# Seven block products for eight in the feed-forward input layers of a two-block model

## The chip, the cores and the metric

One core of a Trainium2 chip runs the whole program. The metric is the device time of one execution in microseconds (us); lower is better. PE is the matmul engine (TensorE), PEld its weight loads, DVE the vector engine (VectorE), ACT the scalar engine, POOL GpSimd, SP the queue that issues the weight transfers.

## The reference

Two model blocks on 512 tokens of width 1024, all in fp32. Each block has mixers (state space, attention, gating; then dilated attention and mLSTM) and feed-forward layers; there are three of these, called f1, f2 and f3 below. All three compute

```python
FF_HIDDEN = 2816
a, b = jnp.split(h @ w_in, 2, axis=-1)      # w_in: 1024 x 5632
f = (jax.nn.silu(a) * b) @ w_out            # w_out: 2816 x 1024
```

## The kernel before

Every fp32 operand of a large product is kept as two fp32r pages, a high half (`hi`, a rounded copy that ACT makes, L300) and a low half (`lo`, what is left, that DVE makes, L306), and each product is three matmuls: high by high (L315), high by low (L316), low by high (L317). That is `mm3`.

`swiglu` runs a feed-forward layer in two parts of 11 groups. A group is one pair of outer tiles: 128 columns of `a` and the 128 columns of `b` that belong to them. `linear_fm` computes a group: the weights come in two slabs (`raw`, 4 tiles of 128 rows by 256 columns, one transfer for each pair member), are split into `whi` and `wlo`, and stand as stationary operand; the 512 tokens of `xT` stream past. A group has 2 outer tiles x 8 row tiles x 3 = 48 matmuls of 512 columns into two PSUM banks. At the start of a layer the first two groups are computed in two passes of 256 tokens each (`half` 0 and 1), since the second half of the tokens is normalized late. At a group's end ACT applies Silu (L901), DVE multiplies (L902), and the result `hid` is split at once (L300, L306). After 11 groups the down-projection (`resid`, by `linear_tm` or, at f1's end, `linear_pairs`) uses `hid` as stationary and streams `w_out`.

Each engine runs its instructions in the order in which the program writes them. `tick` writes one piece of PE work, and after it the evacuations that the piece before left behind; `slab` fetches weights: transfers up to six slabs ahead, splits up to three. SBUF work pages come from a pool of 36, PSUM has 8 banks.

Of the kernel before, what the change touches and what calls it, by code (L numbers as in the profile page):

```python
# [9 lines left out]
F32 = mybir.dt.float32  # L10
F32R = mybir.dt.float32r
# [5 lines left out]
P = 128  # L17
# [64 lines left out]
class Lin:  # L82


    keep = 0

    def __init__(self, w, K, groups, kind, kt, k0=0, rot=0):
        self.w = w.rearrange("(k p) n -> p k n", p=P)
# [7 lines left out]
    def chunks(self):  # L96
        return [(k, min(self.kt, self.KT - k)) for k in range(0, self.KT, self.kt)]

    def specs(self):
        for gi, ents in enumerate(self.groups):  # L100
            n = sum(e[1] for e in ents)
            ch = self.chunks()
            for k, kk in ch[: len(ch) - self.keep] if gi else ch:
# [10 lines left out]
                yield srcs, kk, n, self.rot  # L114


class XT:
# [13 lines left out]

    def __getitem__(self, k):
        return self.tiles[k // 4][:, k % 4]


class LateXT(XT):
# [109 lines left out]
class Core:  # L246
# [5 lines left out]
    def __init__(self, tc, ins, out, dbg=None):  # L252
        self.tc = tc
        self.nc = tc.nc
        self.ins = ins
        self.out = out
        self.dbg = dbg
        self.n = 0
        self.pend = []
        self.bgs = []  # L260
        self.now = 0.0
        self.left = None
        self.specs = []
        self.i_raw = self.i_split = self.i_use = 0
        self.raws, self.splits = {}, {}
        self.los = []

    def nm(self, s):
        self.n += 1
# [55 lines left out]
    def prefetch(self, n_raw, n_split):  # L325
        nc = self.nc
        n_raw, n_split = min(n_raw, len(self.specs)), min(n_split, len(self.specs))
        while self.i_split < n_split or self.i_raw < n_raw:
            if self.i_raw < n_raw and self.i_raw - self.i_split < self.RAW:
                srcs, kt, n, _ = self.specs[self.i_raw]  # L330
                raw = self.page(name="raw")
                rv = raw[:, : kt * n].rearrange("p (k n) -> p k n", k=kt)
                for off, w, ap in srcs:
                    nc.sync.dma_start(rv[:, :, off : off + w], ap)
                self.raws[self.i_raw] = raw
                self.i_raw += 1
            elif self.i_split < n_split:
                i = self.i_split
                srcs, kt, n, rot = self.specs[i]
# [12 lines left out]
                self.i_split += 1  # L352
            else:
                break

    def slab(self, lin, idx, ahead=2):
# [5 lines left out]
        self.i_use += 1  # L362
        return self.splits.pop(i)

    def run_los(self):
        los, self.los = self.los, []
        for f in los:
            f()


    def tick(self, emit, evacs=(), cost=1.0, soon=()):
# [8 lines left out]
        for f in list(soon) + self.pend:  # L380
            f()
        self.pend = list(evacs)
        for b, n in ns:
# [9 lines left out]
            f()  # L393
        self.pend = []

    def linear_fm(self, lin, xT, evac, groups=2):


        idx = 0
# [20 lines left out]
        if self.left:  # L420
# [16 lines left out]
                    )  # L437
            post.finish(range(NT))
            self.left = None
            for gi, ents, ps, ci, k0, kk, hl in work:  # L440
# [5 lines left out]
        for gi in range(first, len(lin.groups)):  # L446
            ents = lin.groups[gi]
            ps = [self.ps("fm") for _ in ents]
            for ci, (k0, kk) in enumerate(ch):
# [4 lines left out]
                for mi, a, n in steps:  # L454
# [3 lines left out]
                        [lambda gi=gi, ps=ps: evac(gi, ps)] if last else (),  # L458
                        cost=n / 4,
                    )  # L460

    def linear_tm(self, lin, xT, evac, tail=2, post=None):

# [3 lines left out]
        for gi, ents in enumerate(lin.groups):  # L467
# [20 lines left out]

            while len(ch) - done > tail:
                k0, kk = ch[done]  # L490
                if isinstance(xT, LateXT):
                    xT.need(k0)
# [4 lines left out]
                done += 1  # L497
            sl = []
            for k0, kk in ch[done:]:
                if isinstance(xT, LateXT):  # L500
                    xT.need(k0)
                sl.append((k0, kk, self.slab(lin, idx)))
                idx += 1
            for t in range(NT):
# [16 lines left out]
    def linear_pairs(self, lin, xT, evac, post):  # L521
# [14 lines left out]
        for p in range(2):  # L536
# [3 lines left out]
            tail = lin.keep if p == 0 else self.TAIL_PAIR  # L540
            sl = []
            for k in ks:
                if p and k >= lin.KT - lin.keep:
                    s = kept[k - lin.KT + lin.keep][1]
                else:
# [253 lines left out]
    def plan_all(self):  # L799
# [3 lines left out]
        def pair(c0, n):  # L803
            return [[(c0 + 256 * g, P), (c0 + 256 * g + P, P)] for g in range(n)]

        def fm(name, w, K, groups, kt=4, k0=0, rot=0):
            L[name] = self.plan(Lin(w, K, groups, "fm", kt, k0, rot))

        def tm(name, w, K, groups, kt=2, k0=0, keep=0):
            L[name] = Lin(w, K, groups, "tm", kt, k0)  # L810
# [6 lines left out]
        def ffn(name, w_in, w_out):  # L817
            for part in range(2):
                j0 = part * nh
                fm(f"{name}i{part}", w_in, D, [[((j0 + j) * P, P), (FFH + (j0 + j) * P, P)] for j in range(nh)])  # L820
# [72 lines left out]

    def swiglu(self, name, xT, h, gain, first, post=None, stats=None):
        nc = self.nc
        for part in range(2):
            hid = []
# [9 lines left out]
            self.linear_fm(self.L[f"{name}i{part}"], xT, ev, self.HALF_F1 if name == "f1" else 2)  # L907
# [5 lines left out]
            self.flush()  # L913

    def rms_post(self, h, gain_row, name, order="same", fp32_out=None):

# [1397 lines left out]
class Block2(Block1):  # L2314
# [14 lines left out]
    FIN1 = 23  # L2329
    MLSTM_RATE = 2.5  # L2330
    HALF_F1 = 2
    PAIRS = ("f1",)
    KEEP = 3
    TAIL_PAIR = 4
# [869 lines left out]
```

## Time and profile before

| | us |
|---|---|
| time, median of 3 runs (lowest, highest) | 2498.6 (2497.31, 2502.82) |
| the profiled execution's own time | 2498.47 |
| its span, first to last instruction | 2496.8 |
| PE busy | 2414.6, 97% |
| DVE busy | 1292.4, 52% |

The time is the span and some 1.7 us around it. PE busy is the time in which a matmul was in the array, and says nothing of how fast matmuls follow each other; that is read from the starts of consecutive rows.

### The profile page before, as it was taken

What the parts mean: (1) busy time and instruction counts of PE and PEld (TensorE: products, weight loads), DVE (VectorE), ACT (ScalarE), POOL (GpSimd) and SP (SyncE); (2) the same over time, 40 slices, a digit from 0 to 9 for tenths busy, and PEclk for the clock granted to TensorE, in tenths of its full rate; (3) what the DMA queues carried; (4) which work ended last, traced back from release to release, by engine and by line L of the source; (5) the groups of instructions that cost most, each with busy time, mean ns of one, the idle gap of its engine ahead of it and who ended that gap; (6) DMA issues with size and microseconds to landing.
All of it is one profiled execution on the core that took longest, in us unless ns stands there. A gap on an engine that the chain in (4) does not pass through costs nothing.

```text
span 2496.8 us, 30987 instructions
## 1 busy us (share of the span) xinstructions
PE 2414.6 (97%) x11960; PEld 1991.2 (80%) x11960; DVE 1292.4 (52%) x2161; ACT 964.4 (39%) x1666; POOL 307.9 (12%) x345
## 2 busy tenths in 40 slices
PE   6989999997999999999999999999999999999998
PEld 5877776677878888888888888888888777888887
DVE  6768736686444367455545563323355566433233
ACT  4345446632221234555445543312233454322231
POOL 2025412104000001121011200000001231000000
PEclk8989999998999999999999999999999999999999
DMA  8255651353333243332333242232241214324321
GB/s 298 83 173 169 212 181 58 119 183 105 110 110 94 80 137 105 93 85 76 110 85 91 88 128 85 89 114 85 85 135 36 58 60 136 100 80 119 88 80 48
DMA packets 330916, 272.79 MB, mean 109 GB/s; under 512 B 28178, under 2 KB 286630, under 8 KB 330768
## 3 DMA queue, kind: packets, MB, share of 16 engines
q1 hardware_dynamic: 323764, 252.36, 33.1%
q0 software_dynamic: 3344, 9.78, 1.1%
q10 hardware_dynamic: 3660, 8.66, 0.9%
q8 instruction: 94, 1.54, 0.3%
q14 instruction: 54, 0.44, 0.1%
HBM read 253.45 MB, written 13.09 MB: 107 GB/s over the span
## 4 chain that ended last, share of the span: by engine, by line
PE 82%; DVE 7%; ACT 2%; issue 1%; POOL 1%; DMA 0%; DVEq 0%; ACTq 0%; POOLq 0%
PE fm L315 17%; PE fm L316 16%; PE fm L317 16%; PE tm L315 8%; PE tm L317 8%; PE tm L316 8%; DVE wlo L306 1%; PE ao L2575 1%; PE as L2449 1%; PE tr L750 1%; PE apt L2551 0%; PE ms L1841 0%; PE mo L1903 0%; DVE rq_t L630 0%; ACT mT L296 0%
## 5 line engine op out<-in xcount | busy, mean ns | idle before, releaser
L315 PE MATMUL fm<-xT,whi 128*128 128x512 f32 (+1 forms) x1744 | 664.6, 381 | 0.3 <-ACT xT L300 0.2
L317 PE MATMUL fm<-xT,wlo 128*128 128x512 f32 (+1 forms) x1744 | 658.5, 378 | 4.4 <-DVE wlo L306 4.4
L316 PE MATMUL fm<-xT,whi 128*128 128x512 f32 (+1 forms) x1744 | 657.3, 377 | 0.8 <-DVE xT L306 0.7
L306 DVE TENSOR_TENSOR wlo<-raw,whi 128x1024 fp32r<-128x1024 f32 (+4 forms) x445 | 488.6, 1133 | 87.8 <-ACT whi L300 69.7
L300 ACT CAST whi<-raw 128x1024 fp32r<-128x1024 f32 (+3 forms) x447 | 393.4, 920 | 143.8 <-PE tm L316 51.1
L317 PEld LDWEIGHTS fm<-xT,wlo 128*128 128x128 f32 x1744 | 331.8, 190 | 66.9 <-DVE wlo L306 4.6
L315 PEld LDWEIGHTS fm<-xT,whi 128*128 128x128 f32 x1744 | 332.5, 191 | 61.5 <-issue 1.7
L316 PEld LDWEIGHTS fm<-xT,whi 128*128 128x128 f32 x1744 | 332.1, 190 | 60.5 <-DVE xT L306 1.4
L902 DVE TENSOR_TENSOR sl<-sl,fm 128x512 f32<-128x512 f32 x66 | 45.4, 688 | 425.5 <-PE fm L317 413.0
L315 PE MATMUL tm<-whi,hid 128*128 128x512 f32 x528 | 208.4, 395 | 0.0
L317 PE MATMUL tm<-whi,hid 128*128 128x512 f32 x528 | 207.7, 393 | 0.0
L316 PE MATMUL tm<-wlo,hid 128*128 128x512 f32 x528 | 207.5, 393 | 0.0
L901 ACT ACTIVATE sl<-fm 128x512 f32<-128x512 f32 x66 | 39.5, 599 | 382.2 <-PE fm L317 382.2
L317 PEld LDWEIGHTS tm<-whi,hid 128*128 128x128 f32 x528 | 99.1, 188 | 23.2
L316 PEld LDWEIGHTS tm<-wlo,hid 128*128 128x128 f32 x528 | 99.2, 188 | 22.8
L315 PEld LDWEIGHTS tm<-whi,hid 128*128 128x128 f32 x528 | 99.1, 188 | 22.8
L315 PE MATMUL tm<-whi,xT 128*128 128x384 f32 (+1 forms) x320 | 114.5, 358 | 0.0
L300 ACT CAST hid<-sl 128x512 fp32r<-128x512 f32 x66 | 41.0, 621 | 187.0 <-DVE sl L902 187.0
L317 PE MATMUL fm<-hT,wlo 128*128 128x512 f32 x256 | 103.9, 406 | 8.5 <-DVE wlo L306 8.5
L317 PE MATMUL tm<-whi,xT 128*128 128x384 f32 (+1 forms) x320 | 112.1, 350 | 0.0
L316 PE MATMUL tm<-wlo,xT 128*128 128x384 f32 (+1 forms) x320 | 111.7, 349 | 0.0
L315 PE MATMUL fm<-hT,whi 128*128 128x512 f32 x256 | 105.3, 411 | 0.3 <-ACT whi L300 0.3
(596 smaller groups left out, 3434.7 us busy)
## 6 DMA issues: line engine op xcount, KB each, us to landing
raw<-in_ffn_w_in_dram SPq DMA_DIRECT2D x264, 256.0 KB, 3.4
raw<-in_ffn_w_out_dram SPq DMA_DIRECT2D x69, 512.0 KB, 3.6
raw<-in_attn_w_in_dram SPq DMA_DIRECT2D x96, 256.0 KB, 3.3
adaw<-in_w_ada_dram SPq DMA_DIRECT2D x40, 512.0 KB, 6.8
raw<-in_w_in_dram SPq DMA_DIRECT2D x36, 512.0 KB, 7.8
raw<-in_attn_w_in_dram SPq DMA_DIRECT2D x96, 128.0 KB, 2.6
raw<-in_mlstm_w_in_dram SPq DMA_DIRECT2D x24, 512.0 KB, 3.7
gates<-gt ACTq DMA_DIRECT2D x12, 512.0 KB, 5.5
```

The lines of the kernel that those rows point to most:

```text
L300: nc.scalar.copy(hi, src)
L306: f = lambda: eng.tensor_tensor(lo, src, hi.bitcast(F32), op=ALU.subtract)
L315: nc.tensor.matmul(out, a[0], b[0], start=start, stop=False)
L316: nc.tensor.matmul(out, a[0], b[1], start=False, stop=False)
L317: nc.tensor.matmul(out, a[1], b[0], start=False, stop=stop)
L750: self.nc.tensor.transpose(ps[:, (k - k0) * P : (k - k0 + 1) * P], src[:, k * P : (k + 1) * P], self.ident)
L901: nc.scalar.activation(s, ps[0], AF.Silu)
L902: nc.vector.tensor_tensor(s, s, ps[1], op=ALU.mult)
L2449: nc.tensor.matmul(ss[:, rs], q[:, rs], k[:, rs], start=True, stop=True)
L2575: nc.tensor.matmul(ov[:, :, r, :], vs[1][:, r, g - 1, :], t3(pts[1 + g][:, rs]), start=g == 1 and r == 0, stop=False,)
```

## The change

36 of the 66 groups are computed in another way: in f1 the groups 4, 6, 8, 10 of the first part and 0, 2, 4, 6, 8, 10 of the second; in f2 and f3 the groups 4, 5, 7, 8, 10 of the first part and 0, 1, 3, 4, 6, 7, 9, 10 of the second. For such a group the weights are four blocks of 512 rows x 128 columns (row half by pair member), the tokens four blocks of 512 rows x 256 tokens. Instead of eight block products there are seven, of sums and differences of blocks (Strassen's scheme in the form with shared sums). Three parts are new:

- `win_prep`, per group: DVE forms the weight sums S1 to S4 in place; ACT and DVE split the seven blocks.
- `win_x`, once per layer: DVE adds the halves of `xT` back together, forms the token sums T1 to T4 and splits them; both parts use them.
- `win_pair`: seven products of 12 matmuls of 256 columns (84 for 48 of 512) in three PSUM banks `wa`, `wb`, `wc`, each bank two halves; DVE adds them up as they finish, ACT applies Silu, DVE multiplies.

The preparations are generators in a list `jobs`; `tick` takes one step of them for each 0.51 of cost, from 1.3 groups ahead. `hid` is kept unsplit (`Hidden`, two groups to a page) and is split in 1024-wide pieces when the down-projection is two pairs away, the first ones during the part's last group. The other 30 groups run as before (`std_group`).

```diff
+    def win_prep(self, i):
+        self.prefetch(i + 4, i + 2)
+        r1, r2 = self.raws.pop(i), self.raws.pop(i + 1)
+        s = self.page(name="ws")
+        q = self.t2(name="wq")
+        v = lambda pg: pg.rearrange("p (m k n) -> p m (k n)", m=2, k=4)
+        v1, v2, vs = v(r1), v(r2), v(s)
+        tt(vs, v2[:, 0].unsqueeze(1).to_broadcast([P, 2, 512]), v1, op=ALU.subtract)
...
+        high("1", r1)
+        yield
+        tt(v2[:, 0], v1[:, 0], vs[:, 1], op=ALU.subtract)
+        tt(q, v2[:, 1], v2[:, 0], op=ALU.subtract)
+        yield
+        low("1", r1)
+        high("2", r2)
+        yield
+        low("2", r2)
+        high("s", s)
+        yield
+        low("s", s)
+        qr = self.page([P, 2, 512], F32R, "wqs")
+        nc.scalar.copy(qr[:, 0], q)
+        yield
+        tt(qr[:, 1], q, qr[:, 0].bitcast(F32), op=ALU.subtract)
...
+    def win_pair(self, i, tx, store):
+        w = self.win.pop(i)
+        a, b, c = self.ps("wa"), self.ps("wb"), self.ps("wc")
...
+        def prod(out, wn, xn):
+            for k in range(4):
+                self.mm3(out, (wh[:, k], wl[:, k]), (xh[:, k], xl[:, k]), k == 0, k == 3)
...
+        def first():
+            nc.scalar.copy(x1, half(b, 0))
+        def sum_11():
+            v(y[:, 0:2], two(a), twice(x1), op=ALU.add)
+        def sum_w():
+            v(y[:, 2], y[:, 1], half(b, 1), op=ALU.add)
+        def sum_22():
+            v(y[:, 1::2], y[:, 1:3], twice(half(b, 0)), op=ALU.add)
+        def out():
+            v(y[:, 1:3], y[:, 1:3], two(c), op=ALU.add)
+            f = y.rearrange("p c n -> p (c n)")
+            nc.scalar.activation(f[:, :512], f[:, :512], AF.Silu)
+            v(store(), f[:, :512], f[:, 512:], op=ALU.mult)
+        seq = [
+            (half(b, 0), "A11", "B11", [first]),
+            (half(a, 1), "S2", "T2", []),
+            (half(a, 0), "A12", "B21", [sum_11]),
+            (half(b, 1), "S3", "T3", [sum_w]),
+            (half(b, 0), "S1", "T1", [sum_22]),
+            (half(c, 0), "S4", "B22", []),
+            (half(c, 1), "A22", "T4", [out]),
+        ]
+        for j, (o, wn, xn, ev) in enumerate(seq):
+            self.tick(lambda: prod(o, wn, xn), ev, cost=0.51)
...
             def ev(gi, ps):
                 s = self.t2(name="sl")
                 nc.scalar.activation(s, ps[0], AF.Silu)
-                nc.vector.tensor_tensor(s, s, ps[1], op=ALU.mult)
-                pg = self.split_page("hid")
-                self.split(pg[:, 0, :], pg[:, 1, :], s)
-                hid.append(pg)
+                nc.vector.tensor_tensor(hid.slot(gi), s, ps[1], op=ALU.mult)
...
+    STD = 4
+    AHEAD = 1.3
+    SEVEN = {
+        "f1": ((4, 6, 8, 10), (0, 2, 4, 6, 8, 10)),
+        "f2": ((4, 5, 7, 8, 10), (0, 1, 3, 4, 6, 7, 9, 10)),
+        "f3": ((4, 5, 7, 8, 10), (0, 1, 3, 4, 6, 7, 9, 10)),
+    }
```

On PE, in f3's second part, the order before runs from the last three matmuls of one slab to the first three of the next group (`fm` is PSUM, `xT` the tokens, `whi` and `wlo` the weights):

```order
L315 MATMUL fm_3032_18663<-xT_2790_16868,whi_3028_18631 128x512
L316 MATMUL fm_3032_18663<-xT_2790_16868,whi_3028_18631 128x512
L317 MATMUL fm_3032_18663<-xT_2790_16868,wlo_3029_18632 128x512
L315 MATMUL fm_3041_18732<-xT_2789_16867,whi_3033_18664 128x512
L316 MATMUL fm_3041_18732<-xT_2789_16867,whi_3033_18664 128x512
L317 MATMUL fm_3041_18732<-xT_2789_16867,wlo_3034_18665 128x512
```

In the changed program, group 6 of that part (counted from 0), the last three matmuls of the first block product and the first three of the second (`wh`, `wl` weights, `wxh`, `wxl` token sums):

```order
L365 MATMUL wb_20510<-xT_18176,wh_20405 128x256
L366 MATMUL wb_20510<-xT_18176,wh_20405 128x256
L367 MATMUL wb_20510<-xT_18176,wl_20439 128x256
L365 MATMUL wa_20509<-wxh_18579,wh_20441 128x256
L366 MATMUL wa_20509<-wxl_18580,wh_20441 128x256
L367 MATMUL wa_20509<-wxh_18579,wl_20443 128x256
```

The three matmuls of `mm3` stay in their order, each now has half the columns, and the bank changes after 12 matmuls instead of 12 or 24 of full width.

On DVE, in f3's second part, before, about two groups:

```order
L902 TENSOR_TENSOR sl_3016_18542<-sl_3016_18542,fm_3002_18453 128x512
L306 TENSOR_TENSOR hid_3017_18545<-sl_3016_18542,hid_3017_18545 128x512
L306 TENSOR_TENSOR wlo_3014_18525<-raw_3000_18424,whi_3013_18524 128x1024
L306 TENSOR_TENSOR wlo_3019_18562<-raw_3005_18457,whi_3018_18561 128x1024
L902 TENSOR_TENSOR sl_3026_18612<-sl_3026_18612,fm_3012_18523 128x512
L306 TENSOR_TENSOR hid_3027_18615<-sl_3026_18612,hid_3027_18615 128x512
L306 TENSOR_TENSOR wlo_3024_18595<-raw_3010_18494,whi_3023_18594 128x1024
```

In the changed program, the stretch that is written while PE computes the unchanged group 5 between two new groups, up to the first row of group 6 (`wy` the block sums, `wl` low halves, `ws`, `raw`, `wq` the weight sums):

```order
L577 TENSOR_TENSOR wy_20312<-wy_20312,wc_20310 128x512
L580 TENSOR_TENSOR hid_20437<-wy_20312 128x512
L447 TENSOR_TENSOR wl_20439<-raw_20286,wh_20405 128x1024
L447 TENSOR_TENSOR wl_20443<-raw_20292,wh_20441 128x1024
L447 TENSOR_TENSOR wl_20459<-ws_20402,wh_20445 128x1024
L465 TENSOR_TENSOR wqs_20461<-wq_20403,wqs_20461 128x512
L436 TENSOR_TENSOR ws_20482<-raw_20399,raw_20331 128x1024
L452 TENSOR_TENSOR raw_20399<-raw_20331,ws_20482 128x512
L453 TENSOR_TENSOR wq_20483<-raw_20399 128x512
L447 TENSOR_TENSOR wl_20501<-raw_20331,wh_20485 128x1024
L447 TENSOR_TENSOR wl_20505<-raw_20399,wh_20503 128x1024
L1167 TENSOR_TENSOR hid_20437<-sl_20526,fm_20422 128x512
```

A group had four rows on DVE; here eleven stand beside one group: the end of the new group before it, the splits of one new group and the sums of the next. The splits of `hid` have left this place.

## Rows read from the trace of the kernel before

**Rows 1.** The page, part 1: busy us, share of span, instructions

```profile
PE 2414.6 (97%) x11960; PEld 1991.2 (80%) x11960; DVE 1292.4 (52%) x2161; ACT 964.4 (39%) x1666; POOL 307.9 (12%) x345
```

**Rows 2.** The page, part 4: the chain that ended last, by engine

```profile
PE 82%; DVE 7%; ACT 2%; issue 1%; POOL 1%; DMA 0%; DVEq 0%; ACTq 0%; POOLq 0%
```

**Rows 3.** Waits of PE in the second feed-forward (who, for whom: us, times, longest)

```profile
PE fm L316 <- DVE xT L306: 0.3, 1, 0.3
PE fm L315 <- ACT xT L300: 0.2, 1, 0.2
```

**Rows 4.** Timeline of ACT: Silu rows ten groups apart, three second parts

```profile
775.60 0.60 ACT L901 ACTIVATE sl<-fm 128x512 f32<-128x512 f32 x1 [21.47 <-PE fm L317]
...
887.01 0.60 ACT L901 ACTIVATE sl<-fm 128x512 f32<-128x512 f32 x1 [6.02 <-PE fm L317]
...
1678.92 0.60 ACT L901 ACTIVATE sl<-fm 128x512 f32<-128x512 f32 x1 [26.91 <-PE fm L317]
...
1790.13 0.60 ACT L901 ACTIVATE sl<-fm 128x512 f32<-128x512 f32 x1 [5.95 <-PE fm L317]
...
2314.46 0.60 ACT L901 ACTIVATE sl<-fm 128x512 f32<-128x512 f32 x1 [26.84 <-PE fm L317]
...
2425.10 0.60 ACT L901 ACTIVATE sl<-fm 128x512 f32<-128x512 f32 x1 [6.00 <-PE fm L317]
```

**Rows 5.** Timeline of PE: first and last row of three runs of 256-column products

```profile
591.58 0.29 PE L316 MATMUL fm<-xT,whi 128*128 128x256 f32 x1
...
603.68 0.39 PE L315 MATMUL fm<-xT,whi 128*128 128x512 f32 x1
...
1499.44 0.28 PE L317 MATMUL fm<-xT,wlo 128*128 128x256 f32 x1
...
1509.52 0.40 PE L315 MATMUL fm<-xT,whi 128*128 128x512 f32 x1
...
2128.47 0.28 PE L316 MATMUL fm<-xT,whi 128*128 128x256 f32 x1
...
2145.25 0.39 PE L315 MATMUL fm<-xT,whi 128*128 128x512 f32 x1
```

**Rows 6.** Busy us (count) by engine, then PEclk and DMA, in stretches

```profile
core 0: us, PE busy (x) PEld busy (x) DVE busy (x) ACT busy (x) POOL busy (x), PEclk, DMA share, GB/s
1498.00:1509.50 11.50, 11.50 (x97) 11.46 (x97) 1.98 (x4) 4.05 (x5) 0.00 (x0) 1.00 0.30 86
2315.00:2425.00 110.00, 110.00 (x479) 89.73 (x478) 36.52 (x40) 29.70 (x39) 0.00 (x0) 1.00 0.27 84
2245.00:2314.00 69.00, 69.00 (x300) 56.03 (x299) 21.83 (x24) 14.72 (x16) 0.00 (x0) 1.00 0.41 118
```

**Rows 7.** DVE by form, 2315 to 2425: count, busy us, mean ns, idle

```profile
L306 DVE TENSOR_TENSOR wlo<-raw,whi 128x1024 fp32r<-128x1024 f32 x20 | 23.5, 1220 | 0.0
L306 DVE TENSOR_TENSOR hid<-sl,hid 128x512 fp32r<-128x512 f32 x10 | 6.9, 693 | 6.9 <-ACT hid L300 6.9
L902 DVE TENSOR_TENSOR sl<-sl,fm 128x512 f32<-128x512 f32 x10 | 6.9, 688 | 68.7 <-PE fm L317 68.7
```

**Rows 8.** Groups of ACT by form, the same stretch

```profile
L300 ACT CAST whi<-raw 128x1024 fp32r<-128x1024 f32 x19 | 19.0, 1045 | 0.0
L300 ACT CAST hid<-sl 128x512 fp32r<-128x512 f32 x10 | 6.2, 622 | 29.6 <-DVE sl L902 29.6
L901 ACT ACTIVATE sl<-fm 128x512 f32<-128x512 f32 x10 | 6.0, 599 | 71.7 <-PE fm L317 71.7
```

**Rows 9.** Groups by form, whole run: 256-wide DVE, and ACT

```profile
L306 DVE TENSOR_TENSOR wlo<-raw,whi 128x256 fp32r<-128x256 f32 x48 | 20.0, 417 | 0.0
L300 ACT CAST whi<-raw 128x256 fp32r<-128x256 f32 x48 | 19.4, 405 | 0.0
```

**Rows 10.** Weight loads by form, 1498 to 1509.5

```profile
L315 PEld LDWEIGHTS fm<-xT,whi 128*128 128x128 f32 x33 | 6.2, 189 | 0.1
```

**Rows 11.** The page, part 6: DMA issues, KB each, us to landing

```profile
raw<-in_ffn_w_in_dram SPq DMA_DIRECT2D x264, 256.0 KB, 3.4
```

More of the change, by code (lines that the diff above doesn't have):

```diff
@@ L133, in __getitem__, with __init__, slot, need @@
         return self.tiles[k // 4][:, k % 4]
+class Hidden:
+    def __init__(self, core):
+        self.core = core
+        self.pages = []
+        self.his = []
+    def slot(self, j):
+        if j % 2 == 0:
+            self.pages.append(self.core.page([P, 2, 512], name="hid"))
+        return self.pages[j // 2][:, j % 2]
+    def need(self, k, n):
+        while len(self.his) <= min(k, n - 1) // 2:
+            j = len(self.his)
+            w = min(2, n - 2 * j)
+            src = self.pages[j][:, :w]
+            hi, lo = (self.core.page([P, 2, 512], F32R, x) for x in ("hidh", "hidl"))
+            self.his.append((hi, lo))
+            self.core.split(hi[:, :w], lo[:, :w], src)
+            self.pages[j] = None
+    def __getitem__(self, k):
+        hi, lo = self.his[k // 2]
+        class Pair:
+            def __getitem__(s, i):
+                return (hi, lo)[i[1]][:, k % 2, i[2]]
+        return Pair()
 class LateXT(XT):
@@ L338, in prefetch @@
                 i = self.i_split
-                srcs, kt, n, rot = self.specs[i]
+                srcs, kt, n, rot, split = self.specs[i]
+                if not split:
+                    self.i_split += 1
+                    continue
                 raw = self.raws.pop(i)
@@ new lines, in std_prep, with win_x, whole, halves @@
+    def std_prep(self, i, n=2):
+        for j in range(n):
+            self.prefetch(i + j + 1 + self.RAW, i + j + 1)
+            yield
+            yield
+    def win_x(self, xT, res):
+        nc = self.nc
+        blk = lambda a, b: tuple(xT.tiles[a][:, :, c, 256 * b : 256 * b + 256] for c in range(2))
+        b11, b12, b21, b22 = (blk(a, b) for a in range(2) for b in range(2))
+        new = lambda: self.page([P, 4, 256], name="wx")
+        def whole(eng, x):
+            pg = new()
+            eng.tensor_tensor(pg, x[0].bitcast(F32), x[1].bitcast(F32), op=ALU.add)
+            return pg
+        def halves(pg):
+            hi = self.page([P, 4, 256], F32R, "wxh")
+            lo = self.page([P, 4, 256], F32R, "wxl")
+            self.split(hi, lo, pg)
+            return hi, lo
+        v = nc.vector
+        x22 = whole(v, b22)
+        x12 = whole(v, b12)
+        yield
+        t1 = whole(v, b11)
+        v.tensor_tensor(t1, x12, t1, op=ALU.subtract)
+        yield
+        v.tensor_tensor(x12, x22, x12, op=ALU.add)
+        yield
+        v.tensor_tensor(x22, x22, t1, op=ALU.add)
+        yield
+        x21 = whole(v, b21)
+        yield
+        v.tensor_tensor(x21, x21, x22, op=ALU.subtract)
+        yield
+        res["T2"] = halves(x22)
+        yield
+        res["T3"] = halves(x12)
+        yield
+        res["T4"] = halves(x21)
+        res["B11"], res["B21"], res["B22"] = b11, b21, b22
+        yield
+        res["T1"] = halves(t1)
+        yield
@@ L382, in tick @@
         self.pend = list(evacs)
+        self.at_group += cost / 4
+        self.turns += cost / 0.51
+        while self.turns >= 1:
+            self.turns -= 1
+            self.job()
         for b, n in ns:
@@ L394, in flush, with std_group, mms, linear_fm @@
         self.pend = []
-    def linear_fm(self, lin, xT, evac, groups=2):
+    def std_group(self, lin, xT, gi, evac):
+        ps = [self.ps("fm") for _ in range(2)]
+        for ci in range(2):
+            hi, lo = self.slab(lin, 2 * gi + ci)
+            for mi in range(2):
+                cs = slice(mi * P, mi * P + P)
+                def mms():
+                    for k in range(4):
+                        xp = xT[4 * ci + k]
+                        self.mm3(
+                            ps[mi], (hi[:, k, cs], lo[:, k, cs]), (xp[:, 0], xp[:, 1]), ci + k == 0, ci == 1 and k == 3
+                        )
+                self.tick(mms, [lambda: evac(gi, ps)] if ci and mi else ())
+    def linear_fm(self, lin, xT, evac, groups=2, upto=None, full=None):
         idx = 0
@@ L445, in linear_fm @@
                 )
-        for gi in range(first, len(lin.groups)):
+        for gi in range(first, len(lin.groups) if upto is None else upto):
             ents = lin.groups[gi]
@@ L819, in ffn @@
                 j0 = part * nh
[L820 removed]
+                ents = [[((j0 + j) * P, P), (FFH + (j0 + j) * P, P)] for j in range(nh)]
+                fm(f"{name}i{part}", w_in, D, ents, raws=self.SEVEN[name][part])
                 if name in self.PAIRS and part == 1:
@@ L895, in swiglu @@
         nc = self.nc
+        tx = {}
         for part in range(2):
-            hid = []
+            hid = Hidden(self)
+            lin = self.L[f"{name}i{part}"]
+            n = len(lin.groups)
+            std = self.STD if part == 0 else 0
             def ev(gi, ps):
@@ L913, in swiglu, with hid_first @@
             self.flush()
+    def hid_first(self, hid, n, i):
+        self.prefetch(i + 4, i + 1)
+        hid.need(1, n)
+        yield
+        yield
+        self.prefetch(i + 5, i + 2)
+        hid.need(3, n)
+        yield
+        yield
     def rms_post(self, h, gain_row, name, order="same", fp32_out=None):
```

115 lines of the change are left out of this document (104 added, 11 removed).

## The prediction

> **What bounds the kernel now.** I read the page first: PE is busy for 97% of the span, DVE for 52% [rows 1], and on the chain that ended last PE holds 82% [rows 2]. That alone does not say that the feed-forward stages hang on PE, so the next view is the waits of PE inside them: in the whole second feed-forward, 366 us, they come to 0.5 us [rows 3]. The third one's list is empty. So in these stages PE starts the next matmul as soon as the last one lets it, everything else lies beside it, and the stage's length is the number of matmuls times their spacing.
>
> The spacing is what the change trades in. A busy row's mean does not give it, since rows of matmuls overlap; starts do. For the full-width group I take the Silu at its end, ten groups apart [rows 4]: (887.01 - 775.60)/10 = 11.14 us in f1, 11.12 in f2, 11.06 in f3, for 48 products of 512 columns, that is 0.231 us each. For 256 columns the trace has the two-pass groups at the head of each layer [rows 5]: 104 spacings in 12.10 us (0.1163) in f1, 85 in 10.08 us (0.1186) in f2 (a small foreign product stands among them), 143 in 16.78 us (0.1173) in f3. Half the columns thus take 0.50 to 0.51 of the time: the short product costs nearly nothing extra. The granted clock is 1.00 (2.4 GHz) in both kinds of stretch [rows 6].
>
> **What the change removes and adds on PE.** 36 groups drop 48 products of 512 columns and take 84 of 256. At 0.1186 us that is 9.96 us a group, at 0.1163 it is 9.77. I take 9.96, the upper one, because a group has edges (new banks, evacuations) that the plain run has not: f3's whole group also is longer than 48 of its running spacings. Saved: f1 10 x (11.14 - 9.96) = 11.8; f2 13 x (11.12 - 9.96) = 15.1; f3 13 x (11.06 - 9.96) = 14.3; together 41 us. With 9.77 it would be 48. With no other change on PE this holds as long as operands, banks and transfers arrive in time, which is the rest of this part.
>
> **DVE.** Prices: 1.22 us for a 1024-wide row, 0.69 for 512 [rows 7], 0.42 for 256 [rows 9]. The strided 512-wide block sum (two pieces of 256 out of PSUM) has no row; its nearest is the 0.69 that reads PSUM too, a 1024-wide row bounds it from above, and two of the 256-wide ones (0.84) lie between. I take 0.69; with 1.22 each new group has 0.5 us more of DVE, which changes nothing below. A new group: one weight sum and three low halves at 1.22; two weight sums, one low half, two block sums, the last addition and the multiply at 0.69; one 256-wide sum: 4 x 1.22 + 7 x 0.69 + 0.42 = 10.1 us. That is over one group of PE time (9.96) by itself. But the unchanged groups that stand between have 2 x 1.22 + 0.69 = 3.1 us against 11.1 of PE (before, each group had 36.52/10 = 3.65 and DVE waited 68.7 us of those 110 for the next group to end [rows 6, 7]). So f2 and f3 (two new, one old) need 23.4 us of DVE in 31.0 of PE, 75%; f1 (one and one) 13.3 in 21.1, 63%. All told DVE gets 36 x 10.1 + 30 x 3.1 + 41 (`hid`) + 44 (`win_x`) - 66 x 3.65 = 301 us more; I cost them at nothing, under the products of the same three groups.
>
> The order says where it is dense: beside the old group eleven rows, 6 x 1.22 + 5 x 0.69 = 10.8 us, and ACT's Silu (0.60 [rows 8]) for which DVE waits between the first two: 11.4 in 11.1 us. What the following new group needs first (three low halves and a fourth) is done after 6.4 us of it; the last two splits are for the group after that, 10 us away. Beside the new group then stand only 5.6 us of DVE, so the lag of 0.3 us does not grow. What is queued behind DVE's waits: a block sum waits for its third, fifth or seventh product, and behind it stand splits for a group that is one group away. PE waits only if DVE is over about 6 us late.
>
> At the head of a layer come `win_x`, 12 x 1.22 = 14.6 us, and the preparation of two new groups. From the second pass of the first two groups to the first new group PE has 96 x 0.117 + 2 x 11.1 = 33.4 us, DVE some 32: twelve rows of `win_x`, three multiplies, three splits, 7.0 and 5.0 us of preparation. What PE needs first, the splits of group 3, is written before most of that, and the last 5 us are for the second new group. Tight, hidden. Without the cover of the first new group's own 10 us it would cost those 5 us once per layer.
>
> The splitting of `hid` moves into the down-projection: 5.5 rows of 1.22 = 6.7 us a part, where DVE has 21.8 us of work in 69 [rows 6]. Nothing on the path: the first two pairs are split while the part's last group runs.
>
> **The others.** ACT: 3 x 1.045 + 0.62 + 0.60 [rows 8] + 0.41 [rows 9] = 4.8 us in 9.96. The copy of the first product frees the half bank that the fifth one overwrites, 4.2 us later (36 products of 0.1186): even behind one split of 1.05 it is in time. Transfers: the same 256 KB pieces, 3.4 us to landing [rows 11], asked for about one group ahead. PSUM: three banks for two; two new groups and an old one hold 3 + 3 + 2 = 8, and the first has long been read by then.
>
> **Sum.** The profiled execution took 2498.47 us, 0.1 from the median of 2498.6, so no correction: 2498.5 - 41.2 = 2457.3, and 1 us for new waits at six seams, where the trace shows 0.5 us a layer now: **2458 us**.
>
> **A row against a rule.** In the 256-column stretch the weight loads are busy for 11.46 of 11.50 us, 0.19 us each [rows 6, 10], and yet the products follow at 0.117: loads run under products. The Trainium skill, "TensorE: Matmul & The Clock Gate", section "The mechanism" of the part on packing, says that a load overlaps a running matmul only when the row groups differ, which they do not here; its section on LDWEIGHTS gives columns over 1.2 GHz, 107 ns for 128. By these a 256-column product would stand at an estimated 214 ns (the load and as long again for 256 columns at 2.4 GHz), a new group at 18.0 us, and the kernel at 2498 + 36 x 6.9 = 2746 us. The trace disagrees, with 117 ns.
>
> **The rivals.**
> (a) Forecast: 36 to 48 us saved, 2450 to 2463.
> (b) Some waiting in the new groups: 0.3 to 1 us each (11 to 36 us), by DVE being late behind the dense stretch. Speaks for it: 75% load and an engine in strict order that waits for PE three times a group. Against: leads of one group. With 0.6 us each: 2457 + 22 = 2479.
> (c) The change does nothing, since waits eat all: 1.15 us a group. 2498. Nothing points to that size in particular.
> (d) Slower: DVE's queue is held. If a block sum is released only when the whole new group ends, DVE stands from product three to product seven, 4 x 1.42 = 5.7 us, and for Silu 1.3: 7 us a new group. Then three groups of f2 and f3 need 23.4 + 14 = 37.4 us for 33.2 before. Thirteen such triples: +55 us; f1 still gains 11: 2498 + 44 = 2542. It decides from (33.2 - 23.4)/2 = 4.9 us held per new group. Against it: the sums stand in the order right behind the products that they read, and such holds overlap with what DVE would idle anyway.
> (e) Slower: the loads stop hiding in long runs. If the spacing were one load's 0.19 us, a group would have 84 x 0.19 = 16.0 us: +4.9 x 36 = +175, 2673. The point is 11.1/84 = 0.132 us. Against: 143 products in a row at 0.117 [rows 5]. (This is the mechanism to which the skill's two rules above belong.)
>
> **How the numbers follow.** Chances: (a) 0.68, (b) 0.20, (c) 0.05, (d) 0.04, (e) 0.01; 0.02 for more than 48 us saved. A measurement of this kernel cannot tell 0.2%, 5 us, from no change. Faster by more than that: (a), (b) and the rest, 0.90; within it 0.05; slower 0.05. The range for 8 in 10 holds (a) and the better part of (b): 2450 to 2477, from the sum with 9.77 us a group to half a microsecond of waiting in each.
>
> **What would show it.** The new products `wa`, `wb`, `wc` (3024 of them) start 0.116 to 0.119 us apart, and the period of a new group is 9.8 to 10.0 us. The waits of PE in the three layers stay under 2 us each. PE's busy time falls by about 40 us, DVE's rises by some 300 to about 1590, ACT's by 80. The down-projections and the mixers keep their lengths. Wrong would be: waits of PE on `wl` or `wqs` inside new groups (b, d), a spacing over 0.12 without waits (e), or a granted clock under 1.00 in these stages, which I gave no case of its own because the 256-column stretches show 1.00.

## The result, and the profile after

The changed kernel takes **2455.9 us** (median of 4 runs, 2453.3 to 2460.2) against 2500.6 for the kernel before beside it (4 runs): ratio 0.982, 95% interval 0.980 to 0.985. The prediction was 2458 us, range 2450 to 2477. The profiled execution took 2453.3 us, its span is 2451.6.

The page's part 1 (busy us, share of the span, instructions) and the engine line of its part 4, which answer to [rows 1, 2]:

```profile
PE 2365.0 (96%) x13256; PEld 2016.0 (82%) x13256; DVE 1566.8 (64%) x2491; ACT 1037.8 (42%) x1756; POOL 306.6 (13%) x345
...
PE 81%; DVE 7%; ACT 2%; issue 1%; POOL 1%; DMA 0%; DVEq 0%; ACTq 0%; SPq 0%; POOLq 0%
```

VectorE does 274 us more and the chain is still TensorE's. Where the time went is read from the timeline of TensorE: the first group-stage product of each part and the first product of the down-projection behind it. For the second part of f2, before:

```profile
1670.44 0.39 PE L315 MATMUL fm<-xT,whi 128*128 128x512 f32 x1
...
1792.77 0.40 PE L315 MATMUL tm<-whi,hid 128*128 128x512 f32 x1
```

After, for the second part of f2 (first row, second row) and of f3:

```profile
1650.60 0.28 PE L365 MATMUL wb<-xT,wh 128*128 128x256 f32 x1
...
1763.21 0.40 PE L365 MATMUL tm<-whi,hidh 128*128 128x512 f32 x1
...
2269.88 0.28 PE L365 MATMUL wb<-xT,wh 128*128 128x256 f32 x1
...
2382.43 0.39 PE L365 MATMUL tm<-whi,hidh 128*128 128x512 f32 x1
```

Read in the same way, all six parts (us to the down-projection, in first parts from the first 512-column product behind the 256-column run, in second parts from the first product):

| stage | before | after | change | new groups |
| --- | --- | --- | --- | --- |
| f1 first, second | 101.6, 122.6 | 97.1, 116.7 | -4.5, -5.8 | 4, 6 |
| f2 first, second | 99.9, 122.3 | 93.8, 112.6 | -6.1, -9.7 | 5, 8 |
| f3 first, second | 99.6, 121.8 | 94.3, 112.6 | -5.4, -9.2 | 5, 8 |

Together -40.7 us. From the first 256-column product of f1 (at 560.0 before, 555.8 after) to the end it is 1936.8 against 1895.8, -41.0. The 4.2 us ahead of that point are code that both kernels share; in the runs below the point lies between 555.1 and 564.9, so this is scatter, and lengths from there (**the length from f1**) are what I compare below beside the times.

One pair of new groups in f2, on TensorE's timeline, from the first product of the pair to the eight-product group behind it:

```profile
1681.50 0.28 PE L365 MATMUL wb<-xT,wh 128*128 128x256 f32 x1
...
1691.43 0.28 PE L365 MATMUL wb<-xT,wh 128*128 128x256 f32 x1
...
1701.38 0.40 PE L365 MATMUL fm<-xT,whi 128*128 128x512 f32 x1
```

168 products in 19.88 us: 0.1183 us each, 9.94 a group, as in [rows 5]. TensorE's waits in the three feed-forwards (who, for whom: us, times, longest), against [rows 3]: in f1, 555 to 955,

```profile
PE tr L1008 <- DVE h L2536: 8.7, 2, 7.1
PE fm L367 <- DVE wlo L356: 4.4, 1, 4.4
PE tr L1008 <- DVE xn L2603: 2.2, 2, 1.7
PE wb L365 <- ACT wx L562: 1.6, 1, 1.6
```

in f2 the 0.5 us of before, in f3 none. Before, the same part of f1 had the first two of these too:

```profile
PE tr L750 <- DVE h L2233: 9.2, 3, 7.1
PE fm L317 <- DVE wlo L306: 4.4, 1, 4.4
```

Only the last row of f1 is a wait inside a new group: TensorE holds the `wb` bank's next product until ACT has copied the group's first product out of it. The timelines of ACT and PE show why the copy was late:

```profile
784.54 0.63 ACT L989 ACTIVATE tab<-rq 64x512 f32<-64x512 f32 x1 [3.03 <-DVE rq L988]
785.18 0.60 ACT L1166 ACTIVATE sl<-fm 128x512 f32<-128x512 f32 x1
785.67 0.37 ACT L562 COPY wx<-wb 128x256 f32<-128x256 f32 x1
786.09 0.39 PE L365 MATMUL wb<-wxh,wh 128*128 128x256 f32 x1 [1.58 <-ACT wx L562]
```

ACT stood 3.03 us for VectorE at a row of the rotary tables, code that both kernels have at this place; a Silu and the copy came behind it. It looks like nothing here; the experiments come back to it.

VectorE by form, whole run (count, busy us, mean ns, idle before), against [rows 7]:

```profile
L447 DVE TENSOR_TENSOR wl<-raw,wh 128x1024 fp32r<-128x1024 f32 x72 | 85.2, 1219 | 0.0
L447 DVE TENSOR_TENSOR wl<-ws,wh 128x1024 fp32r<-128x1024 f32 x36 | 43.9, 1219 | 0.1
L436 DVE TENSOR_TENSOR ws<-raw,raw 128x1024 f32<-128x1024 f32 x36 | 43.9, 1219 | 0.0
...
L566 DVE TENSOR_TENSOR wy<-wa,wx 128x512 f32<-128x512 f32 x36 | 24.8, 689 | 28.4 <-PE wa L367 19.6 <-issue 8.8
L573 DVE TENSOR_TENSOR wy<-wy,wb 128x512 f32<-128x512 f32 x36 | 24.7, 687 | 1.2
```

The strided block sum `wy<-wy,wb`, which no trace of before had, takes 0.687 us, the value I took. And 72 rows of 1.219 us are busy for 85.2 us, not 87.8: neighbouring rows overlap.

### The profile page after: what moved, and what is told of

It reads as the page before. It is cut to its first block, busy times and chain, and to the rows that moved or that the text cites. A ratio compares the mean times of both kernels' runs of the same rounds, so it can differ in the third digit from the quotient of the medians.

```text
span 2451.6 us, 34170 instructions
## 1 busy us (share of the span) xinstructions
PE 2365.0 (96%) x13256; PEld 2016.0 (82%) x13256; DVE 1566.8 (64%) x2491; ACT 1037.8 (42%) x1756; POOL 306.6 (13%) x345
## 4 chain that ended last, share of the span: by engine, by line
PE 81%; DVE 7%; ACT 2%; issue 1%; POOL 1%; DMA 0%; DVEq 0%; ACTq 0%; SPq 0%; POOLq 0%
PE fm L365 12%; PE fm L366 11%; PE fm L367 11%; PE tm L366 8%; PE tm L365 8%; PE tm L367 8%; PE wb L365 2%; PE wb L366 2%; PE wb L367 2%; PE wc L366 1%; PE wc L367 1%; PE wc L365 1%; PE wa L366 1%; PE wa L365 1%; PE wa L367 1%; DVE wlo L356 1%
## 5 line engine op out<-in xcount | busy, mean ns | idle before, releaser
L356 DVE TENSOR_TENSOR wlo<-raw,whi 128x1024 fp32r<-128x1024 f32 (+3 forms) x373 | 408.9, 1120 | 166.1 <-ACT whi L350 71.5
L365 PE MATMUL fm<-xT,whi 128*128 128x512 f32 (+1 forms) x1168 | 436.6, 374 | 0.3 <-ACT xT L350 0.2
L367 PE MATMUL fm<-xT,wlo 128*128 128x512 f32 (+1 forms) x1168 | 430.6, 369 | 4.4 <-DVE wlo L356 4.4
L366 PE MATMUL fm<-xT,whi 128*128 128x512 f32 (+1 forms) x1168 | 430.8, 369 | 0.8 <-DVE xT L356 0.7
L350 ACT CAST whi<-raw 128x1024 fp32r<-128x1024 f32 (+4 forms) x375 | 325.8, 897 | 143.9 <-PE tm L367 43.5
L367 PEld LDWEIGHTS fm<-xT,wlo 128*128 128x128 f32 x1168 | 223.2, 191 | 41.9 <-DVE wlo L356 4.7
L365 PEld LDWEIGHTS fm<-xT,whi 128*128 128x128 f32 x1168 | 223.4, 191 | 36.9 <-issue 1.5
L366 PEld LDWEIGHTS fm<-xT,whi 128*128 128x128 f32 x1168 | 223.2, 191 | 34.4 <-DVE xT L356 1.5
L366 PE MATMUL tm<-wlo,hidh 128*128 128x512 f32 x528 | 208.0, 394 | 0.4 <-DVE wlo L356 0.4
L365 PE MATMUL tm<-whi,hidh 128*128 128x512 f32 x528 | 208.4, 395 | 0.0
L367 PE MATMUL tm<-whi,hidl 128*128 128x512 f32 x528 | 207.9, 394 | 0.0
L366 PEld LDWEIGHTS tm<-wlo,hidh 128*128 128x128 f32 x528 | 99.2, 188 | 23.5 <-DVE wlo L356 0.9
L365 PE MATMUL fm<-hT,whi 128*128 128x512 f32 x256 | 104.0, 406 | 0.0
L366 PE MATMUL fm<-hT,whi 128*128 128x512 f32 x256 | 101.8, 398 | 0.0
```

The lines of the kernel that those rows point to most:

```text
L350: nc.scalar.copy(hi, src)
L356: f = lambda: eng.tensor_tensor(lo, src, hi.bitcast(F32), op=ALU.subtract)
L365: nc.tensor.matmul(out, a[0], b[0], start=start, stop=False)
L366: nc.tensor.matmul(out, a[0], b[1], start=False, stop=False)
L367: nc.tensor.matmul(out, a[1], b[0], start=False, stop=stop)
```

## The experiments

Each run's ratio is to runs of the kernel before on the same chip (medians 2497.7 to 2502.0 us).

**1. The change without its products.** All groups in the old form; only the late splitting of `hid` stays.

```diff
-        "f1": ((4, 6, 8, 10), (0, 2, 4, 6, 8, 10)),
+        "f1": ((), ()),        # f2, f3 alike; no win_x
```

> No group is computed with seven products and no token sums are made; what is left of the change is that hid is kept whole and split in 1024-wide pieces during the down-projection. My theory (the gain is matmul time in the 36 groups and nothing else): as before the change, 2497 to 2503, the feed-forward groups at 11.06 to 11.14 us each. Rival (part of the gain comes from moving and merging the splits of hid): 2480 to 2493.

Measured: 2499.1 us, ratio 1.0005 (0.999 to 1.002), length from f1 1938.7 (1936.8 before). The new layout of `hid` is free; the whole gain is that of the groups.

**2. Fewer products.** The sixth product takes half of its rows (S4 times B22 is left half undone).

```diff
-            for k in range(4):
-                self.mm3(out, (wh[:, k], wl[:, k]), (xh[:, k], xl[:, k]), k == 0, k == 3)
+            n = 2 if wn == "S4" else 4
+            for k in range(n):
+                self.mm3(out, (wh[:, k], wl[:, k]), (xh[:, k], xl[:, k]), k == 0, k == n - 1)
```

> The sixth product of each new group (S4 times B22) takes 2 of its 4 blocks of 128 rows, so 6 of 84 products of 256 columns are left out in 36 groups; nothing else changes. Theory (the group's time is the number of its products times 0.1175 us, and VectorE has room in the triples): 36 x 6 x 0.1175 = 25.4 us less than the changed kernel, 2429 to 2434 us. Rival (VectorE's 10.1 us per new group is the floor under a group of 9.2 us): pairs stay near 19.8 us and the time is above 2440 us.

Measured: 2436.9 us (2430.7 to 2438.8), ratio 0.976; length from f1 1874.8, 21.0 less than the changed kernel. The stage shows it more sharply. Timeline of TensorE, second part of f2 in this kernel:

```profile
1647.88 0.28 PE L365 MATMUL wb<-xT,wh 128*128 128x256 f32 x1
...
1754.50 0.39 PE L365 MATMUL tm<-whi,hidh 128*128 128x512 f32 x1
```

106.6 us for 112.6: 6.0 us for 8 x 6 products, 0.125 each. The six parts lose 25.0 us, for the 25.4 that was expected. The time missed its 2429 to 2434 by 3 us; in the profiled execution (2438.3 us) f1 began 6 us later and the attention layer ahead of f3 took 3.4 us longer, code that the edit does not touch. VectorE is no floor under 9.2 us groups in pairs: a group's price is its number of products.

**3. All groups of f2 and f3 new.** Without eight-product groups between, VectorE has 10.1 us of rows for each 9.94.

```diff
-        "f2": ((4, 5, 7, 8, 10), (0, 1, 3, 4, 6, 7, 9, 10)),
+        "f2": ((4, 5, 6, 7, 8, 9, 10), (0, 1, 2, 3, 4, 5, 6, 7, 8, 9, 10)),   # f3 alike
```

> In f2 and f3 every group from 4 on in the first part and all of the second part take seven products, ten more than in the changed kernel. My theory (VectorE's 10.1 us a group and its wait for Silu are hidden only because an old group stands between): without old groups VectorE needs 10.9 to 11.4 us a group, PE waits for low halves in those groups, and the time is 2453 to 2480, no gain over the changed kernel. Rival (PE alone sets the pace): 2456 - 10 x 1.15 = 2444.

Measured: 2456.7 us, ratio 0.984 (0.981 to 0.986): no gain, though it saves ten more groups' worth of products. The time lies in the expected range, but the way to it was another: no product of a new group waits for a low half. First parts fall to 92.2 and 92.6 us, but the second parts stay at 112.5, 10.23 us a group. Between 1680 and 1760 no matmul is listed as waiting, but the weight loads are:

```profile
PEld wb L365 <- ACT wx L562: 1.7, 7, 0.3
```

The windows of the same stretch (us, then PE, PEld, DVE, ACT, POOL busy, clock, DMA share, GB/s):

```profile
1680.00:1760.00 80.00, 79.68 (x661) 78.27 (x660) 71.59 (x92) 33.26 (x47) 0.00 (x0) 1.00 0.33 100
```

0.2 to 0.3 us in each group, before the fourth product, on the same copy as the wait in f1. ACT's timeline ahead of one of them:

```profile
1696.79 0.63 ACT L579 ACTIVATE wy<-wy 128x512 f32<-128x512 f32 x1 [5.98 <-DVE wy L577]
1697.32 1.03 ACT L441 CAST wh<-raw 128x1024 fp32r<-128x1024 f32 x1
1698.26 0.37 ACT L562 COPY wx<-wb 128x256 f32<-128x256 f32 x1
```

ACT stands for the last block sum of the group before, then does its Silu and a cast, and only then the copy.

**4. Help from GpSimd.** As 3, with one of the four low halves (raw less high, 1024 wide) on GpSimd.

```diff
-            tt(lo, pg, hi.bitcast(F32), op=ALU.subtract)
+            eng = nc.gpsimd if key == "1" else nc.vector
+            eng.tensor_tensor(lo, pg, hi.bitcast(F32), op=ALU.subtract)
```

> As the run with all groups of f2 and f3, and the low half of the first weight page of each new group is made on GpSimd. My theory: VectorE then has 8.9 us a group plus the wait for Silu, just under PE's 9.9, so that PE waits little and the ten groups give 10 us: 2444 to 2450. Rival (GpSimd and VectorE hold each other up, or GpSimd's 2.4 us a row come too late for the first product): PE waits for wl, 2456 or more.

Measured: 2474.1 us, ratio 0.991 (0.988 to 0.993), 17 us slower than 3. Timeline:

```profile
1700.72 2.38 POOL L448 TENSOR_TENSOR wl<-raw,wh 128x1024 fp32r<-128x1024 f32 x1 [9.22 <-ACT wh L441]
1700.96 2.70 DVE L466 TENSOR_TENSOR wqs<-wq,wqs 128x512 fp32r<-128x512 f32 x1
```

VectorE's 512-wide row, 0.68 us elsewhere, takes 2.70: it ends 0.56 us after GpSimd's row does. In the second part of f2 the `wqs` rows have a mean of 1.90 us. The 1.14 us taken off VectorE come back as up to 2 us of standing. TensorE pays for it at the copy again, and not at a low half from GpSimd: its waits there, 3.4 us in 3, are now (whole run)

```profile
PE wb L365 <- ACT wx L563: 25.2, 23, 3.5
```

The Trainium skill, "SBUF — State Buffer", section "Who interferes with whom", says that a VectorE instruction with two SBUF inputs contends with a GpSimd instruction that reads SBUF; this row agrees.

**5. More VectorE work.** The changed kernel, with its first weight sum written three times (2.44 us more per new group).

```diff
-        tt(vs, v2[:, 0].unsqueeze(1).to_broadcast([P, 2, 512]), v1, op=ALU.subtract)
+        for _ in range(3):
+            tt(vs, v2[:, 0].unsqueeze(1).to_broadcast([P, 2, 512]), v1, op=ALU.subtract)
```

> The first weight sum of each new group is written three times over on VectorE, which adds 2 x 1.22 us to it in each of the 36 groups, 88 us in all. My theory (that work is hidden up to about 31 us in three groups of f2 and f3): 28.2 us of work and 1.6 us for two waits on Silu still fit 30.9, so 2454 to 2464. Rival (VectorE is at its limit, its work shows): up to 2456 + 88 = 2544, and in any case over 2475.

Measured: 2486.3 us, ratio 0.995 (0.993 to 0.997); length from f1 1922.8, 27 us more than without. My theory of "about 6 us" of slack fell. TensorE's waits, whole run:

```profile
PE wb L365 <- ACT wx L563: 18.8, 10, 3.4
```

The timeline around one of them:

```profile
1695.24 3.73 DVE L437 TENSOR_TENSOR ws<-raw,raw 128x1024 f32<-128x1024 f32 x3
...
1699.01 0.70 DVE L453 TENSOR_TENSOR raw<-raw,ws 128x512 f32<-128x512 f32 x1
...
1699.78 1.05 ACT L442 CAST wh<-raw 128x1024 fp32r<-128x1024 f32 x1 [5.84 <-issue]
...
1700.73 1.04 ACT L442 CAST wh<-ws 128x1024 fp32r<-128x1024 f32 x1
...
1701.68 0.59 ACT L1167 ACTIVATE sl<-fm 128x512 f32<-128x512 f32 x1
...
1702.17 0.61 ACT L464 CAST wqs<-wq 128x512 fp32r<-128x512 f32 x1
...
1702.68 0.37 ACT L563 COPY wx<-wb 128x256 f32<-128x256 f32 x1
...
1703.10 0.39 PE L365 MATMUL wb<-wxh,wh 128*128 128x256 f32 x1 [1.86 <-ACT wx L563]
```

The longer weight sum ends late, the next one (`raw`) with it; the cast on ACT that reads it starts at 1699.78, and behind it in ACT's order stand another cast, a Silu, a third cast and then the copy of the first product, which had been there to copy since 1698.4. TensorE stands 1.9 us. The idle time of the cast is put down to "issue", but it starts just behind VectorE's row that writes its input. The expectation of the next run names another chain, over the last sum and its Silu (L580); eight of the ten waits go over the weight sums and the casts, as here, one (0.83 us) over that Silu, and one (3.37 us) over the rotary tables in f1.

VectorE's share in three triples (a triple is one eight-product group and two new ones) of this run; the columns are those of the windows in 3:

```profile
1673.80:1764.00 90.20, 85.66 (x583) 78.69 (x582) 75.72 (x88) 29.36 (x40) 0.00 (x0) 1.00 0.31 93
```

It is 84%, and TensorE is busy for 85.66 us of the 90.20.

**6. Which product waits.** My first reading of 5 was that the fifth product waits, which overwrites the half bank that is copied. So: a bank of its own for the fifth product, with 5's extra sums, and with all groups new.

```diff
-            (half(b, 0), "S1", "T1", [sum_22]),
+            (half(d, 0), "S1", "T1", [sum_22]),      # d = self.ps("wd"); sum_22 reads it
```

> The first weight sum of each new group is again written three times (2.44 us more of VectorE per new group, as in the run of 2486 us), but the fifth product of a group goes to a PSUM bank of its own instead of into the half bank of the first, so that TensorE no longer waits there for ScalarE's copy of the first product. Theory (the 30 us came over one chain: VectorE late, the last sum late, Silu held, the copy held behind it in ScalarE's queue, fifth product held): the waits of the wb tiles on ScalarE's copy, 18.8 us in all, vanish, pairs go back to about 19.9 us, and the time is 2455 to 2468 us. Rival (VectorE with 12.5 us of work per 9.9 us group is itself the bound, and another wait, for the low halves or the sums, takes the place): at least 2480 us.

> The second and third feed-forward layers have all their groups new, as in the run of 2456.7 us, and the fifth product has its own PSUM bank. There the second parts took 10.23 us per group with 9.0 us of VectorE busy in each. Theory (the same chain over Silu and ScalarE's copy makes the 0.3 us): 9.9 to 10.0 us per group, 3 us less in each of two second parts, 2449 to 2453 us. Rival (VectorE's in-order queue sets the pace by its own work and its 0.7 us wait for Silu, which the bank doesn't touch): 10.2 us per group again and 2455 to 2459 us.

Measured: 2478.5 us, ratio 0.993 (0.991 to 0.996), and 2454.8 us, ratio 0.984 (0.981 to 0.986), second parts of 112.1 us. Both theories fell on the bank that they freed. Waits of the first of the two, whole run:

```profile
PE wb L365 <- ACT wx L563: 15.4, 10, 3.4
```

One of them on TensorE's timeline:

```profile
1696.30 0.39 PE L365 MATMUL wb<-wxh,wh 128*128 128x256 f32 x1 [1.65 <-ACT wx L563]
```

This group began at 1690.3; three products on is 1694.6, so it is the fourth that waits, as at 1703.10 in 5 (begun at 1696.85). The fourth writes the other half of the bank. The copy is thus due not three products after the first ends, but two: 2.8 us, not 4.2.

**7. The first product in its own bank.** This frees the fourth; first with 5's extra sums.

```diff
-            nc.scalar.copy(x1, half(b, 0))
+            nc.scalar.copy(x1, half(d, 0))
...
-            (half(b, 0), "A11", "B11", [first]),
+            (half(d, 0), "A11", "B11", [first]),
```

> The run with the fifth product in a bank of its own kept 15.4 us of waits on ScalarE's copy, and its trace shows them before the fourth product of a group (it writes the other half of the bank from which the copy reads), not before the fifth. So here the first weight sum is written three times as before (2.44 us more VectorE per new group), and the first product alone has its own bank. Theory (VectorE late by its weight sums, casts of high halves late, the copy queued behind them on ScalarE, the fourth product held): the waits on the copy vanish, pairs take 19.8 to 20.2 us instead of 21 to 24.6, and the time is 2455 to 2466 us. Rival (VectorE late makes another wait, for the low halves or for a free bank, in its place): above 2472 us.

Measured: 2454.8 us, ratio 0.982 (0.980 to 0.985); length from f1 1893.6. No wait on the copy is left in the run, and all 27 us of 5 are gone, with the same VectorE rows. Windows of three triples (columns as in 3):

```profile
1671.00:1764.00 93.00, 93.00 (x651) 86.55 (x650) 82.45 (x95) 33.96 (x46) 0.00 (x0) 1.00 0.34 100
```

VectorE is busy for 89% here and TensorE loses nothing.

**8. Where VectorE does bind.** As 7, with the first weight sum written five times.

> The changed kernel's set of new groups, the first product in its own PSUM bank, and the first weight sum written five times (4.88 us more VectorE per new group, 15.0 us for each). With two more sums (12.5 us) TensorE lost nothing. Theory (with that wait gone TensorE waits only where VectorE's work fills the stretch): a triple has 2 x 15.0 + 3.2 = 33.2 us of VectorE in 30.9 us of TensorE, 2 us over, so some 12 triples of the second and third layers give 20 to 35 us: 2472 to 2492 us, with the stretches of f1 (one new and one eight-product group, 18 us in 21) unchanged. Rival (VectorE's lateness is absorbed by the down-projections and the lead of the preparation, since those stretches end after 2 to 4 triples): under 2465 us.

Measured: 2489.2 us, ratio 0.995 (0.994 to 0.997). TensorE's waits, whole run:

```profile
PE wd L367 <- DVE wl L448: 20.0, 16, 2.9
```

The window of a triple that takes 34.3 us:

```profile
1716.60:1750.90 34.30, 31.50 (x219) 29.02 (x218) 31.90 (x37) 11.09 (x16) 0.00 (x0) 1.00 0.32 93
```

VectorE is busy for 31.9 us of 34.3 and waits for Silu for 1.5 more: it sets the pace, and TensorE now waits for low halves. This is the third triple of its part; the first two take 31.7 and 33.2 us, for the 33.2 expected. f1's stretches kept their 21.0 us for two groups but for one, 24.2 us, with a wait of 2.9 us for a low half. The theory held.

**9. The better versions.** More new groups: 10 of 11 in the second parts of f2 and f3, without and with 7's bank, and all groups with it.

> The second and third layers have all 7 groups of their first part new (10.01 us each in the run with all groups new, 1.7 us less per part than the changed kernel) and 10 of 11 of their second part (one eight-product group in the middle, so that VectorE can catch up). Theory (a run of five new groups leaves VectorE 1.5 us late at 0.3 us per group, under the 2.9 us of slack): second parts of 10 x 9.9 + 11.1 = 110.1 us against 112.5, and 2 x (1.7 + 2.4) = 8 us less than the changed kernel: 2446 to 2451 us. Rival (every run of more than two new groups is paced by VectorE at 10.2 us): 10 x 10.2 + 11.1 = 113 us, and 2453 to 2457 us.

> As the run with all groups of the first parts and 10 of 11 of the second parts new (second parts of 111.7 and 112.0 us there, with one 1.2 us wait on the copy in each), with the first product in its own bank. Theory: the wait on the copy goes, second parts of 110.2 to 110.6 us, 1 us more than with all groups new if those run at 9.9 us: 2448 to 2453 us. Rival (VectorE is the pace of long runs of new groups): the eight-product group lets VectorE catch up, so this one is 1 to 2 us faster than the version with all groups new.

> All groups of the second and third layers new, and the first product of each group in its own PSUM bank. Where all groups were new each group of the second parts lost 0.33 us, and the trace shows it before the fourth product, in the weight load that waits for ScalarE's copy. Theory (VectorE, with 9.0 us of work and 0.7 us of waiting for Silu per group, fits into 9.9 us, and only the copy's place in the queue held TensorE): 9.9 to 10.0 us per group, second parts of 109 to 110 us against 112.5, time 2447 to 2452 us. Rival (VectorE sets 10.2 us per group and the wait moves to another product): 112 us again and 2454 to 2459 us.

| new groups in f2, f3 (first, second part) | bank of 7 | us | ratio | length from f1 | second parts |
| --- | --- | --- | --- | --- | --- |
| 5, 8 (the change) | no | 2455.9 | 0.982 | 1895.8 | 112.6, 112.6 |
| 7, 10 | no | 2457.2 | 0.985 (0.982 to 0.987) | 1893.9 | 111.7, 112.0 |
| 7, 11 | no | 2456.7 | 0.984 | 1893.3 | 112.5, 112.4 |
| 7, 10 | yes | 2451.9 | 0.980 (0.979 to 0.982) | 1886.9 | 110.1, 110.2 |
| 7, 11 | yes | 2447.0 | 0.979 (0.977 to 0.980) | 1882.8 | 109.0, 109.0 |

Without the bank the seventh and tenth new groups bring 2 us from f1 and nothing in the time; the theory for 7, 10 fell (2446 to 2451 expected). With it each costs 9.9 us again, in a run of eleven too, and the version with all groups new is the fastest: 13 us less from f1 than the change, 1.9 of them in f1's second part (114.8 us for 116.7), which loses its one wait on the copy. Both theories with the bank held. Windows of that stretch in it:

```profile
1655.00:1755.00 100.00, 100.00 (x850) 100.00 (x849) 90.06 (x116) 40.98 (x58) 0.00 (x0) 1.00 0.35 103
```

VectorE fits: 8.9 us of work and 0.7 of waiting for Silu per 9.9 us group. So 10.23 in 3 was not VectorE's own pace, as I then thought, but the copy again.

## Why the prediction was right, step by step

**TensorE.** Saved in the groups: 40.7 us, forecast 41.2. That the sum is so near is in part luck: f1 gave 10.3 us for 11.8 (its second part lost 1.6 to the wait on the copy), f2 15.8 for 15.1 and f3 14.6 for 14.3. The medians differ by 44.7 us, with an interval of 39 to 49, so they agree with the sum but cannot test it as closely as the stages do. The spacing from the 256-column runs carried over to 168 products in a row (0.118), the period is 9.94 for the 9.96 taken, and busy time fell by 49.6, where 40 was said. Of these, 5.3 lie ahead of f1, in code that both kernels share; the other 44.3 are the time in which some matmul's row was running, and the ends of such rows are modelled, so lengths are the better measure. Experiment 2 moved the count alone and the time followed it.

**New waits.** 1.6 us in f1, nothing in f2 and f3; 1 us was taken. The sign "under 2 us each" holds for these new waits alone: f1's whole list is 17.6 us, 14.5 of them there before. The down-projections and mixers kept their lengths to within 1.4 us, and experiment 1 shows the split of `hid` to be free.

**VectorE.** Hidden, as forecast: a triple has 22.35 us of it in 31.0 (23.4 forecast). The sum of +301 us came out as +274. It put in the new rows at their durations but took off the old groups at their busy time (3.65 us for four rows of 3.82 in all, 11 us in 66 groups). In durations VectorE's rows come to 1372.0 us before and 1663.2 after, 291 more, and 17 of these lie under neighbouring rows (two 1.22 us rows start 1.14 apart). The rows of before had shown this: 20 rows of 1220 ns, busy for 23.5 us [rows 7]. ACT's busy time rose by 73 us, for 80.

**The copy, where the reasoning was wrong.** "The copy of the first product frees the half bank that the fifth one overwrites, 4.2 us later ... in time" and "PE waits only if DVE is over about 6 us late" both failed, at a cost of 1.6 us here, in f1. The fourth product waits, because the program guards the bank as a whole: the copy reads one half, the product writes the other. The Trainium skill, "PSUM — Partial Sum Buffer", section "PSUM bank collisions raise a hardware error", has the rule: guard PSUM by bank and 32-partition quadrant, or more simply by bank, but not by address. The products here take all 128 partitions, so only another bank helps. The rule would have put the wait in the right place ahead of the run; 6 and 7 agree, in that a new bank helped for the first product and hardly for the fifth. In the changed kernel the margin was thin in f2, too. The timeline of ACT and PE in the last group of f2:

```profile
1755.82 1.04 ACT L350 CAST hidh<-hid 128x1024 fp32r<-128x1024 f32 x1
...
1756.77 0.36 ACT L562 COPY wx<-wb 128x256 f32<-128x256 f32 x1
...
1757.55 0.28 PE L365 MATMUL wb<-wxh,wh 128*128 128x256 f32 x1
```

The copy ends 0.42 us before the fourth product starts. Rival (b), some waiting in the new groups behind a late VectorE, was so the nearest of the rivals: 2.44 us more per group made it true (5), through ACT's queue and the bank; TensorE's waits for low halves in new groups come to 0.3 us there, and to 20.0 only in 8.

**The other rivals.** (c): nothing eats the gain. (d): VectorE waits for products without harm, 53 us in all ahead of the 256-wide block sums. (e): the weight loads are busy for 100.0 of 100 us in the last window above, and 256-column products still follow at 0.118: loads do hide. The prediction took the stricter of two sentences in the section "The mechanism" of the Trainium skill's "TensorE: Matmul & The Clock Gate"; the paragraph above it also lets a load run ahead into a background weight buffer. The trace agrees with that one in its effect, 849 loads under 850 products in those 100 us; the buffer itself no run here shows.

## What to carry to other kernels

Where an engine's waits in a stage are near zero, the count of its instructions times the spacing of such instructions elsewhere in the same trace prices a rewrite well: 40.7 us for 41.2 here, and each layer to within 1.5. For what runs beside it, a share of busy time (89% was harmless in 7, 84% was not in 5) says less than the shortest deadline in the chain: look for a small operation that another engine waits for, ask what stands ahead of it in its own queue, and count the deadline from the first access to the whole PSUM bank. One more bank for it was worth 10 us once the groups were denser, and 29 with VectorE's extra sums.

## What the runs showed of the hardware that was not expected

A tensor-tensor row of VectorE, 0.68 us alone, took 2.70 us beside one of GpSimd, and both read two SBUF operands: offloading 1.2 us of work per group cost the kernel 17 us. In the whole run of 4, which of the two began first decided it. All 40 such rows of VectorE that began under a GpSimd row ended behind it, by 0.55 us (512 wide) or 1.08 us (1024 wide); 22 that began first kept their durations, and the GpSimd row ended 2.25 us or more behind them; the 48 block sums beside a GpSimd row, which read PSUM, kept theirs.

A row of VectorE that does not touch what the row ahead wrote starts 0.08 us before that row ends. One that reads it or writes it again starts 0.03 us behind its end: three repeated sums into one page take 3.73 us, five 6.26, 1.25 each.
